# Conv-branch eviction and gate steps re-placed, final norm rearranged, in a one-core hybrid decoder layer

## Chip, core and metric

The program runs on one core of one Trainium2 chip. The metric is device time in microseconds (us) of one execution; lower is better. All 256 tokens (plus 16 learned meta tokens, 272 rows) go through one layer of width 2048 in one launch.

## What is computed

Cut to what matters here, the reference is:

```python
s = concat([meta, x])                                   # 272 x 2048
s = s + 0.5 * swiglu_ffn(rms_norm(s, g1), w_gu, w_down)
h = rms_norm(s, g_mix)
q, k, v, b_gate, c_gate, u = split(h @ w_in)
y_att  = diff_attention(q, k, v, ...)
y_conv = b_gate * short_conv(c_gate * u, conv_w)        # 3 taps along the tokens
z = [y_att @ w_branch[0], y_conv @ w_branch[1]]
s = s + (sum(sigmoid(h @ w_gate) * z)) @ w_out
s = s + 0.5 * swiglu_ffn(rms_norm(s, g2), w_gu, w_down)
out = rms_norm(s, norm_final)[16:]                      # 256 x 2048, fp32
```

## The kernel before, in words

Every large product is done in three fp32r products on TensorE (PE): each weight block is loaded by a DMA (`st`), cast to a high part `wh` on ScalarE (ACT, line 275 or 378), and the rest `wl = st - wh` is formed on VectorE (DVE, line 276 or 379). PE multiplies `wh` with the activation's high and low part and `wl` with its high part. `wh` and `wl` have three buffers each, `st` five. One block is two chunks of 128 rows in `linear` (line 248) and one chunk in `linear_tok` (line 314).

`linear` and `linear_tok` run a list of chunks. What else has to be done is put between the chunks by lists: `pending` holds the eviction of the product before and is emptied after chunk `EVICT_AT = 1` (`flush`); `side` holds small steps, one of which is taken at each chunk of `side_at`; `after` is called after each chunk. The order in which the text calls these is not yet the order on an engine: the framework schedules the instructions, and each engine then runs its own queue strictly in the order of the built program.

The part around the change:

- Lines 842 to 873, the conv branch in two groups `g` of 512 columns. For each group three `linear` calls run: `c`, `u`, `b`, eight blocks each, with `side_at=(3, 6, 9, 12)`. `c` and `u` have 258 token columns and three products per weight tile (lines 287 to 289); `b` has 256 and two (line 285 with 512 columns for both activation parts, line 289 with 256).
- `u_evict` (line 851) multiplies `u` into `cg` and forms the three taps into `yv`: per column tile `j` one multiplication (853), one scaling (855), two multiply-adds (857), four tiles in all, 16 DVE instructions. It runs at the flush in `b`.
- `side` holds the attention at that time: 18 steps of units (`scores`, `turn`, `values`), the norm and eight `att_out` steps (lines 800 to 813: two transposes on PE, line 808, a scaling on DVE, line 809; after every fourth tile a `split` of `yf` into `ya`, lines 173 and 174).
- `hg.renorm` (line 435) makes the activation of the gate from the residual `s`: two DVE instructions (440), then `pair`: an ACT copy (450), a DVE subtraction (451), and for pairs of kind `S` four DVE sums (455 to 458), an ACT copy (460) and a DVE subtraction (461). In group 1 it is called in `u` and `b` after chunks 3, 7, 11 and 15.
- Lines 927 to 992, the final norm. `down` (975) runs for each token half `i` and column quarter (`u`, `q`): add to `sT` (978), square with a sum into `fss` (982, ACT), multiply by the gain (983). In the last `linear_tok` (`hold = 3`) the products of half 1 come last. After the fourth quarter of a half, `finish(i)` (930) sums the four squares (933), scales (935), forms the inverse root by `rsqrt` (lines 222 to 230, the root on ACT) and scales the two column halves, one on ACT (941) and one on DVE (943), each followed by a store of 128 x 1024 issued by SyncE (SP, 944).

Of the kernel before, what the change touches and what calls it, by code (L numbers as in the profile page):

```python
# [22 lines left out]
GC = 4  # L23
GW = GC * P
W2 = D // 2
NH = 8
HD = 64
EPS = 1e-6
# [17 lines left out]
def decoder_layer(ctx: ExitStack, tc: tile.TileContext, t, out):  # L46
    nc = tc.nc

    const = ctx.enter_context(tc.tile_pool(name="const", bufs=1))
# [8 lines left out]
    def wide(shape, name):  # L58
        return tmp.tile(shape, F32, tag="wide", bufs=4, name=name)
# [31 lines left out]
    G_MIX, G_FFN2, G_CONV, G_SUB = 0, DC, 2 * DC, NV - 1  # L91

    def load_gain(g0, src):
# [5 lines left out]
        out=vrows[G_CONV:G_SUB, :], in_=t["conv_w"][0].rearrange("k (c p) -> (k c) p", p=P)  # L99
# [3 lines left out]
    for i, n in enumerate(("lambda_q1", "lambda_k1", "lambda_q2", "lambda_k2")):  # L103
# [7 lines left out]
        out=mask[:, T - P :],  # L111
        in_=mask[:, T - P :],
# [13 lines left out]
    def col(i):  # L126
        return vec[:, i : i + 1]
# [94 lines left out]
    def rsqrt(out_, ms, shape, name):  # L222

        a = tmp.tile([P, T], F32, tag="rsa", bufs=1, name="rsa" + name)[:, : shape[1]]
        nc.scalar.activation(a, ms, AF.Sqrt)
        nc.vector.reciprocal(out_, a)
        nc.vector.tensor_mul(a, out_, out_)
        nc.vector.tensor_mul(a, a, ms)
        nc.vector.tensor_scalar(a, a, -0.5, 1.5, op0=ALU.mult, op1=ALU.add)
        nc.vector.tensor_mul(out_, out_, a)  # L230
# [4 lines left out]
    side = []  # L235
# [174 lines left out]
    def gated_plain(norm, m, gi):  # L410


        def f(acc):
            mt = wide([P, 2, GW], "mt")
            for i in range(2):
                r = norm.rtok[:, i : i + 1]
                silu = tmp.tile([P, GW], F32, tag="sc", name="silu")
                nc.scalar.activation(silu, acc[i][0], AF.Silu, scale=r)
                nc.vector.scalar_tensor_tensor(
                    out=mt[:, i, :], in0=acc[i][1], scalar=r, in1=silu, op0=ALU.mult, op1=ALU.mult  # L420
                )
            for k in range(2):
                later.append(lambda k=k: back(m, 2 * gi + k, mt, k))

        return f
# [413 lines left out]
    nu = T - n0  # L839
    yc = Act("yc", NH, SEQ)  # L840
    hg = Mixed(norm2, G_MIX)
    for g in range(2):
        cg = wide([P, GC, T], "cg")
        yv = apool.tile([P, GC, SEQ], F32, tag="act", name=f"yv{g}")

        def c_evict(ps, cg=cg):
            for j in range(GC):
                nc.vector.tensor_mul(cg[:, j, :nu], ps[j][:, :nu], norm2.rstd[:, n0:])
                nc.vector.tensor_mul(cg[:, j, :nu], cg[:, j, :nu], norm2.rstd[:, n0:])

        def u_evict(ps, cg=cg, yv=yv, g=g):
            for j in range(GC):
                nc.vector.tensor_mul(cg[:, j, :nu], ps[j][:, :nu], cg[:, j, :nu])
                taps = [col(G_CONV + k * NH + g * GC + j) for k in range(3)]
                nc.vector.tensor_scalar_mul(yv[:, j, :], cg[:, j, 0:SEQ], taps[0])
                for k in (1, 2):
                    nc.vector.scalar_tensor_tensor(
                        out=yv[:, j, :], in0=cg[:, j, k : k + SEQ], scalar=taps[k], in1=yv[:, j, :],
                        op0=ALU.mult, op1=ALU.add,
                    )  # L860

        def b_evict(ps, yv=yv, g=g):
            for j in range(GC):
                nc.vector.tensor_mul(yv[:, j, :], yv[:, j, :], norm2.rstd[:, NMETA:])
                nc.vector.tensor_mul(yv[:, j, :], total(ps[j], SEQ), yv[:, j, :])
            split(yc, g, yv)

        kw = dict(side_at=(3, 6, 9, 12))
        linear(h2, allk, w_in, 0, 4 * W2 + g * GW, n0, T, "c", c_evict, **kw)
        for i, (m0, t0, nm, evict) in enumerate(((5 * W2, n0, "u", u_evict), (3 * W2, NMETA, "b", b_evict))):  # L870
            if g == 1:
                kw["after"] = lambda k, i=i: hg.renorm(4 * i + k // 4) if k % 4 == 3 else None
            linear(h2, allk, w_in, 0, m0 + g * GW, t0, T, nm, evict, **kw)
    while side:
        side.pop(0)()
# [26 lines left out]
    sT = [[apool.tile([P, W2], F32, tag="act", name=f"sT{i}{q}") for q in range(2)] for i in range(2)]  # L902
# [27 lines left out]
    def finish(i):  # L930

        ssq = const.tile([P, 1], F32, name=f"fssq{i}")
        nc.vector.tensor_reduce(out=ssq, in_=fss[:, i, :], axis=AX.X, op=ALU.add)
        fms = const.tile([P, 1], F32, name=f"fms{i}")
        nc.vector.tensor_scalar(fms, ssq, 1.0 / D, EPS, op0=ALU.mult, op1=ALU.add)
        fr = const.tile([P, 1], F32, name=f"fr{i}")
        rsqrt(fr, fms, [P, 1], f"f{i}")
        for q in range(2):
            y = sT[i][q]
            if q:  # L940
                nc.scalar.mul(y, y, fr)
            else:
                nc.vector.tensor_scalar_mul(y, y, fr)
            nc.sync.dma_start(out=out[i * P : (i + 1) * P, q * W2 : (q + 1) * W2], in_=y)

    w_gu, w_down = t["ffn2_w_gu"][0], t["ffn2_w_down"][0]
    hn = Mixed(norm3, G_FFN2)
# [8 lines left out]
    for half in thirds:  # L956
        m = Act("m", len(half) * GC, SEQ)
        for gi, g in enumerate(half):
            if g == 0:
                linear_tok(  # L960
                    [(h3, 0, w_gu, 0), (h3, 0, w_gu, F)], allk, 0, "pg", gated_plain(norm3, m, gi),
                    side_at=range(16), after=renorm_after,
                )
            else:
                gate_up_mix(hn, w_gu, g, m, gi)
        final = half is thirds[-1]
        if final:
            for q in range(2):
                nc.gpsimd.dma_start(
                    out=gfin[q],  # L970
                    in_=t["norm_final"][q * W2 : (q + 1) * W2].rearrange("(o d) -> o d", o=1).to_broadcast([P, W2]),
                )
        for u in range(2):

            def down(i, q, ps, u=u, final=final):
                fs = slice(q * GW, (q + 1) * GW)
                v = sT[i][u][:, fs]
                nc.vector.scalar_tensor_tensor(out=v, in0=ps, scalar=0.5, in1=v, op0=ALU.mult, op1=ALU.add)
                if final:
                    k = u * 2 + q  # L980
                    sq = wide([P, GW], "fsq")
                    nc.scalar.activation(sq, v, AF.Square, accum_out=fss[:, i, k : k + 1])
                    nc.vector.tensor_mul(v, v, gfin[u][:, fs])
                    if k == 3:
                        finish(i)

            hold = HOLD if final and u else 0
            linear_tok(
                [(m, 0, w_down, u * W2 + q * GW) for q in range(2)], list(range(len(half) * GC)), half[0] * GC, "pd",
                down if hold else lambda acc, down=down: [down(i, q, acc[i][q]) for q in range(2) for i in range(2)],  # L990
                hold=hold,
            )
# [26 lines left out]
```

## Time and profile before

| | |
|---|---|
| time, median of 3 runs | 2208.49 us (2207.37 to 2209.04) |
| the profiled execution's own time | 2207.09 us |
| its span, first to last instruction | 2205.3 us |
| PE busy | 2187.7 us (99%) |
| DVE busy | 1467.6 us (67%) |
| ACT busy | 1042.1 us (47%) |
| mean granted TensorE clock | 0.998 |

The profiled execution lies 1.8 us above its span; that part is outside the first and last instruction. A row of the timeline has start in us from the span's start, duration, engine, line, operation, output and inputs, a count where equal neighbours are merged, and in brackets how long the engine had been idle and what released it. "PEclk" is the TensorE clock that was granted, 1.00 being full. SPq is the queue in which SP issues DMAs.

### The profile page before, as it was taken

To read this page: it belongs to the slowest core of one execution; us is meant where nothing else is said; L and a number is where in the kernel's file an instruction comes from. 1 tells how busy PE (TensorE), PEld (TensorE's weight loads), DVE (VectorE), ACT (ScalarE), POOL (GpSimd) and SP (SyncE) were. 2 spreads that over 40 slices of the span, in tenths; PEclk is the share of its full clock that TensorE was granted. 3 is DMA by queue.
4 is the path that set the end of the run, shared out by engine and by line. 5 is a ranking of instruction groups with operands and counts; after the bars stand their busy time and mean duration, and the time that the engine had idled before them with its cause. 6 is when DMAs were issued, how large, how long until landed. Compare 5 with 4: busy or idle time off the path is not lost.

```text
span 2205.3 us, 33210 instructions
## 1 busy us (share of the span) xinstructions
PE 2187.7 (99%) x13534; PEld 1974.6 (90%) x13534; DVE 1467.6 (67%) x1903; ACT 1042.1 (47%) x1299; POOL 6.4 (0%) x17
## 2 busy tenths in 40 slices
PE   9999999999999999999999999999999999999997
PEld 8999999999999999898988888888888888888886
DVE  7555554445555565567787777678886688846985
ACT  6343433334333443444555555455554455534554
POOL 0000000000000000000000000000000000000000
PEclk9999999999999999999999999999999999999999
DMA  8555555555555555444535656554566455665562
GB/s 272 173 173 172 175 177 179 177 172 173 173 175 176 181 175 172 157 150 134 173 134 205 214 192 215 186 186 143 195 220 210 158 201 203 222 209 184 181 226 96
DMA packets 192105, 401.96 MB, mean 182 GB/s; under 512 B 8660, under 2 KB 8848, under 8 KB 191952
## 3 DMA queue, kind: packets, MB, share of 16 engines
q1 hardware_dynamic: 191232, 398.49, 53.3%
q8 instruction: 105, 1.72, 0.3%
q0 software_dynamic: 544, 1.21, 0.2%
q14 instruction: 48, 0.39, 0.0%
q10 hardware_dynamic: 176, 0.14, 0.0%
HBM read 397.71 MB, written 2.10 MB: 181 GB/s over the span
## 4 chain that ended last, share of the span: by engine, by line
PE 96%; DVE 1%; ACT 1%; DMA 1%; issue 0%; SPq 0%; DVEq 0%; ACTq 0%
PE pg L487 5%; PE pg L485 5%; PE pg L486 5%; PE pu L289 4%; PE pd L289 4%; PE pd L287 4%; PE pu L287 4%; PE pd L288 4%; PE pu L288 4%; PE pg L289 4%; PE pg L287 4%; PE pg L288 4%; PE pd L329 4%; PE pd L327 4%; PE pd L328 4%; PE o L285 3%
## 5 line engine op out<-in xcount | busy, mean ns | idle before, releaser
L276 DVE TENSOR_TENSOR wl<-st,wh 128x1024 fp32r<-128x1024 f32 x392 | 479.0, 1224 | 454.5 <-ACT wh L275 453.9
L275 ACT CAST wh<-st 128x1024 fp32r<-128x1024 f32 x392 | 411.2, 1050 | 607.3 <-PE pd L288 146.9
L378 ACT CAST wh<-st 128x1024 fp32r<-128x1024 f32 (+1 forms) x360 | 359.2, 1004 | 379.1 <-PE pd L328 128.7
L379 DVE TENSOR_TENSOR wl<-st,wh 128x1024 fp32r<-128x1024 f32 (+1 forms) x360 | 414.2, 1157 | 136.9 <-ACT wh L378 136.5
L287 PE MATMUL pg<-h,wh 128*128 128x272 f32 x704 | 202.9, 289 | 0.8 <-ACT wh L275 0.7
L287 PE MATMUL pu<-h,wh 128*128 128x272 f32 x704 | 203.1, 289 | 0.0
L289 PE MATMUL pd<-m,wl 128*128 128x272 f32 x704 | 203.0, 288 | 0.0
L289 PE MATMUL pu<-h,wl 128*128 128x272 f32 x704 | 203.0, 288 | 0.0
L287 PE MATMUL pd<-m,wh 128*128 128x272 f32 x704 | 202.9, 288 | 0.0
L288 PE MATMUL pu<-h,wh 128*128 128x272 f32 x704 | 202.4, 288 | 0.0
L288 PE MATMUL pd<-m,wh 128*128 128x272 f32 x704 | 202.4, 287 | 0.0
L288 PE MATMUL pg<-h,wh 128*128 128x272 f32 x704 | 201.7, 287 | 0.0
L289 PE MATMUL pg<-h,wl 128*128 128x272 f32 x704 | 200.6, 289 | 0.9 <-DVE wl L276 0.9
L485 PE MATMUL pg<-wh,hn 128*128 128x512 f32 x390 | 152.8, 392 | 0.0
L486 PE MATMUL pg<-wh,hn 128*128 128x512 f32 x390 | 151.9, 390 | 0.0
L487 PE MATMUL pg<-wl,hn 128*128 128x512 f32 x390 | 151.8, 392 | 0.0
L327 PE MATMUL pd<-wh,m 128*128 128x512 f32 x352 | 137.6, 391 | 0.0
L328 PE MATMUL pd<-wh,m 128*128 128x512 f32 x352 | 137.0, 389 | 0.0
L379 DVE TENSOR_TENSOR wl<-tt,wh 128x1024 fp32r<-128x1024 f32 x84 | 101.3, 1222 | 53.7 <-ACT wh L378 50.0
L329 PE MATMUL pd<-wl,m 128*128 128x512 f32 x352 | 136.9, 390 | 0.0
L287 PEld LDWEIGHTS pg<-h,wh 128*128 128x128 f32 x704 | 132.2, 188 | 1.4 <-ACT wh L275 1.4
L288 PEld LDWEIGHTS pg<-h,wh 128*128 128x128 f32 x704 | 132.8, 189 | 0.0
(299 smaller groups left out, 4729.3 us busy)
## 6 DMA issues: line engine op xcount, KB each, us to landing
st<-in_ffn_w_gu_dram SPq DMA_DIRECT2D x184, 512.0 KB, 4.3
st<-in_ffn_w_down_dram SPq DMA_DIRECT2D x88, 1024.0 KB, 5.1
st<-in_ffn_w_gu_dram SPq DMA_DIRECT2D x84, 1024.0 KB, 4.9
st<-in_w_in_dram SPq DMA_DIRECT2D x48, 1024.0 KB, 5.1
st<-in_w_gate_dram SPq DMA_DIRECT2D x64, 512.0 KB, 4.4
st<-in_w_branch_dram SPq DMA_DIRECT2D x32, 512.0 KB, 4.8
st<-in_w_out_dram SPq DMA_DIRECT2D x16, 1024.0 KB, 5.0
xin<-in_x_dram SPq DMA_DIRECT2D x8, 256.0 KB, 8.1
```

The lines of the kernel that those rows point to most:

```text
L275: nc.scalar.copy(out=wh[:, :m, :], in_=sw)
L276: nc.vector.tensor_sub(wl[:, :m, :], sw, wh[:, :m, :].bitcast(F32))
L287: nc.tensor.matmul(a, wh[:, i, f], act.part(c, 0, t0, t1), start=first, stop=False)
L288: nc.tensor.matmul(a, wh[:, i, f], act.part(c, 1, t0, t1), start=False, stop=False)
L289: nc.tensor.matmul(a, wl[:, i, f], act.part(c, 0, t0, t1), start=False, stop=last)
L327: nc.tensor.matmul(ps, hi, wh[:, q, :], start=first, stop=False)
L328: nc.tensor.matmul(ps, lo, wh[:, q, :], start=False, stop=False)
L378: nc.scalar.copy(out=wh, in_=src)
L379: nc.vector.tensor_sub(wl, src, wh.bitcast(F32))
L485: nc.tensor.matmul(ps[k], hi, wh, start=first, stop=False)
L486: nc.tensor.matmul(ps[k], lo, wh, start=False, stop=False)
L487: nc.tensor.matmul(ps[k], hi, wl, start=False, stop=left[k] == 0)
```

## The change

1. `u_evict` does column tiles 0 and 1 at the flush, and puts tiles 2 and 3 at the front of `side`, so that they are taken at chunk 3 of `b`, in the place of the attention step that stood there. All later steps of `side` move back by one slot in each group.
2. `hg.renorm` is called after chunks 4, 7, 10 and 13, for the same pairs in the same order.
3. Final norm: the sum of three of the four quarters and its scaling are done after the third quarter (`finish_part`); after the fourth, one instruction adds its part. A root of one column is taken early, in the eviction of the linear before (`k == 1`, half 1). The product of the last quarter with the gain goes to a new tile `fy`. The chain after the root has one instruction less in front of the scaling on DVE, which takes two scalars. Half 1 is scaled and stored in four pieces of 128 x 512 in place of two of 128 x 1024; those scaled on ACT are issued from ACT's queue.

```diff
         def u_evict(ps, cg=cg, yv=yv, g=g):
-            for j in range(GC):
-                nc.vector.tensor_mul(cg[:, j, :nu], ps[j][:, :nu], cg[:, j, :nu])
...
+            def taps(j0):
+                for j in (j0, j0 + 1):
+                    nc.vector.tensor_mul(cg[:, j, :nu], ps[j][:, :nu], cg[:, j, :nu])
...
+            taps(0)
+            side.insert(0, lambda: taps(2))
...
-                kw["after"] = lambda k, i=i: hg.renorm(4 * i + k // 4) if k % 4 == 3 else None
+                kw["after"] = lambda k, i=i: hg.renorm(4 * i + k // 3 - 1) if k in (4, 7, 10, 13) else None
...
+    fpart = const.tile([P, 2], F32, name="fpart")
+    fr = const.tile([P, 2, 4], F32, name="fr")
+
+    def finish_part(i):
+
+        nc.vector.tensor_reduce(out=fr[:, i, 3:4], in_=fss[:, i, 0:3], axis=AX.X, op=ALU.add)
+        nc.vector.tensor_scalar(fpart[:, i : i + 1], fr[:, i, 3:4], 1.0 / D, EPS, op0=ALU.mult, op1=ALU.add)
+
+    def finish(i, last):
+
+        ms, a, r, n = (fr[:, i, k : k + 1] for k in range(4))
+        nc.vector.tensor_scalar(ms, fss[:, i, 3:4], 1.0 / D, fpart[:, i : i + 1], op0=ALU.mult, op1=ALU.add)
+        nc.scalar.activation(a, ms, AF.Sqrt)
+        nc.vector.reciprocal(r, a)
+        nc.vector.scalar_tensor_tensor(out=n, in0=r, scalar=ms, in1=r, op0=ALU.mult, op1=ALU.mult)
+        nc.vector.tensor_scalar(n, n, -0.5, 1.5, op0=ALU.mult, op1=ALU.add)
+        nc.vector.tensor_mul(a, r, n)
+        rows = out[i * P : (i + 1) * P, :]
+        for u, q in ((0, 1), (0, 0), (1, 0), (1, 1)) if i else ((0, None), (1, None)):
+            cs = slice(0, W2) if q is None else slice(q * GW, (q + 1) * GW)
+            on_act = q == 0 or (q is None and u == 0)
+            y = last if u and q else sT[i][u][:, cs]
+            if on_act:
+                nc.scalar.mul(y, y, a)
             else:
-                nc.vector.tensor_scalar_mul(y, y, fr)
-            nc.sync.dma_start(out=out[i * P : (i + 1) * P, q * W2 : (q + 1) * W2], in_=y)
+                nc.vector.tensor_scalar(y, y, r, n, op0=ALU.mult, op1=ALU.mult)
+            eng = nc.scalar if on_act and i else nc.sync
+            eng.dma_start(out=rows[:, u * W2 + cs.start : u * W2 + cs.stop], in_=y)
...
-                    nc.vector.tensor_mul(v, v, gfin[u][:, fs])
+                    y = wide([P, GW], "fy") if k == 3 and i else v
+                    nc.vector.tensor_mul(y, v, gfin[u][:, fs])
+                    if k == 1 and i:
+
+                        nc.scalar.activation(fr[:, i, 3:4], fss[:, i, 1:2], AF.Sqrt)
+                    if k == 2:
+                        finish_part(i)
                     if k == 3:
-                        finish(i)
+                        finish(i, y)
```

More of the change, by code (lines that the diff above doesn't have):

```diff
@@ L851, in u_evict @@
         def u_evict(ps, cg=cg, yv=yv, g=g):
-            for j in range(GC):
[L853 to L860, printed above, removed]
+            def taps(j0):
+                for j in (j0, j0 + 1):
+                    nc.vector.tensor_mul(cg[:, j, :nu], ps[j][:, :nu], cg[:, j, :nu])
+                    w = [col(G_CONV + k * NH + g * GC + j) for k in range(3)]
+                    nc.vector.tensor_scalar_mul(yv[:, j, :], cg[:, j, 0:SEQ], w[0])
+                    for k in (1, 2):
+                        nc.vector.scalar_tensor_tensor(
+                            out=yv[:, j, :], in0=cg[:, j, k : k + SEQ], scalar=w[k], in1=yv[:, j, :],
+                            op0=ALU.mult, op1=ALU.add,
+                        )
+            taps(0)
+            side.insert(0, lambda: taps(2))
         def b_evict(ps, yv=yv, g=g):
```

11 lines of the change are left out of this document (removed).

## The prediction, made before the changed kernel was run

> **What bounds the kernel now.** I read the page's busy shares first, then PE's waits, then the timeline around the longest wait, then the end of the span.
>
> ```profile
> PE 2187.7 (99%) x13534; PEld 1974.6 (90%) x13534; DVE 1467.6 (67%) x1903; ACT 1042.1 (47%) x1299; POOL 6.4 (0%) x17
> ```
> ```profile
> PE b L289 <- DVE wl L276: 2.3, 1, 2.3
> PE pg L289 <- DVE wl L276: 0.9, 2, 0.6
> ```
> PE is busy all the time, so only PE's idle time, its clock and what lies behind its last product can be won or lost. One wait stands out: in `b` a product waits 2.3 us for a `wl`. No other wait behind the start is longer than 0.6 us. The timeline around it (PE, DVE and ACT rows):
>
> ```profile
> 1097.04 1.05 ACT L275 CAST wh<-st 128x1024 fp32r<-128x1024 f32 x1 [2.05 <-PE u L288]
> 1098.13 1.23 DVE L276 TENSOR_TENSOR wl<-st,wh 128x1024 fp32r<-128x1024 f32 x1 [1.88 <-ACT wh L275]
> 1101.04 0.69 DVE L451 TENSOR_TENSOR hn<-hnf,hn 128x512 fp32r<-128x512 f32 x1
> 1101.35 1.05 ACT L275 CAST wh<-st 128x1024 fp32r<-128x1024 f32 x1
> 1101.65 0.69 DVE L461 TENSOR_TENSOR sp<-sums,sp 128x512 fp32r<-128x512 f32 x1
> 1101.80 0.28 PE L287 MATMUL u<-h,wh 128*128 128x258 f32 x1
> 1102.25 0.76 DVE L853 TENSOR_TENSOR cg<-u,cg 128x258 f32<-128x258 f32 x2
> 1102.76 0.28 PE L289 MATMUL u<-h,wl 128*128 128x258 f32 x1
> 1102.89 0.39 PE L285 MATMUL b<-h,wh 128*128 128x512 f32 x1
> 1105.68 1.10 PE L285 MATMUL b<-h,wh 128*128 128x512 f32 x4
> 1107.80 1.22 DVE L276 TENSOR_TENSOR wl<-st,wh 128x1024 fp32r<-128x1024 f32 x1
> 1109.07 0.74 PE L289 MATMUL b<-h,wl 128*128 128x256 f32 x4 [2.29 <-DVE wl L276]
> ```
> ```profile
> 1106.78:1109.07 2.29, 0.00 (x1) 0.00 (x1) 2.29 (x5) 0.09 (x1) 0.00 (x0) 1.00 0.00 0
> 1110.14:1113.55 3.41, 3.41 (x13) 2.82 (x12) 3.41 (x6) 1.41 (x3) 0.00 (x0) 0.50 0.84 299
> 1113.55:1117.00 3.45, 3.45 (x21) 3.03 (x20) 2.67 (x6) 1.63 (x2) 0.00 (x0) 1.00 0.89 299
> ```
> The windows have length, then busy us of PE, PEld, DVE, ACT and POOL, then granted clock, DMA share and GB/s. DVE works without a pause from 1101.04: a renorm's rest, then the whole `u_evict` from 1102.25 to 1107.80 (5.55 us), and only then the `wl` of `b`'s second block. PE stands for 2.29 us, and shortly after runs 3.41 us at half the clock, which loses half of that, 1.71. Together **4.0 us**. The count of products agrees: eight pairs take 1105.68 - 1102.89 = 2.79 us, 0.349 each; the twelfth pair of `b`'s second and third block would start at 1105.68 + 11 x 0.349 = 1109.52 and starts at
>
> ```profile
> 1113.64 0.40 PE L285 MATMUL b<-h,wh 128*128 128x512 f32 x1
> ```
> that is 4.1 later. The end of the span:
>
> ```profile
> 2193.76 1.28 ACT L225 ACT_TABLE_LOAD   x1
> 2194.38 0.68 DVE L978 SCALAR_TENSOR_TENSOR sT<-pd,sT 128x512 f32<-128x512 f32 x1
> 2195.16 0.61 ACT L982 ACTIVATE fsq<-sT 128x512 f32<-128x512 f32 x1
> 2195.68 0.19 ACT L982 ACTIVATION_READ_ACCUMULATOR fsq<-sT 128x1 f32 x1
> 2196.61 0.15 DVE L933 TENSOR_REDUCE fssq<-fss 128x1 f32<-128x4 f32 x1
> 2196.73 0.75 DVE L943 TENSOR_SCALAR sT<-sT,fr 128x1024 f32<-128x1024 f32 x1
> 2197.51 3.08 SPq L944 DMA_DIRECT2D out_dram<-sT  x4
> 2198.97 1.15 ACT L941 ACTIVATE sT<-sT,fr 128x1024 f32<-128x1024 f32 x1 [1.00 <-DVE fr L230]
> 2199.75 0.84 SPq L944 DMA_DIRECT2D out_dram<-sT  x2
> ```
> ```profile
> 2198.37:2203.71 5.34, 0.00 (x0) 0.00 (x0) 1.23 (x4) 1.15 (x1) 0.00 (x0) 0.56 0.98 393
> ```
> From 2198.37 to 2203.71 the DMA engines are 98% busy: 2.10 MB go out in one unbroken stream of 5.34 us, although the last store is issued only near 2200.2. So the end is set by **when the first store starts** (2197.51, 0.86 before the stream) and by the stream's length, not by the chain of half 1.
>
> **The change part by part.**
>
> *u_evict in two parts, renorm moved.* No work goes; DVE's order changes. In the order of the changed program tiles 2 and 3 stand right behind tiles 0 and 1: the split leaves no gap in DVE's queue. What moves is the `wl` of `b`'s second block: renorm and `ya` no longer stand ahead of it, so it comes *before* `u_evict`, and the third block's `wl` comes behind. I lay this out from t, the start of `b`. A block of `u` has 24 products of 0.12 us (1101.80 to 1102.76 is eight of them), 2.88. The cast of `b`'s second block waits for a buffer that PE frees when the last block of `u` begins, at t - 2.80; cast 1.05, `wl` 1.23, so `u_evict` can start at t - 0.57. It takes 5.55, and the third `wl` runs from t + 4.98 to t + 6.20, seen by PE at t + 6.25. PE begins the third block at t + 5.58 and in the new order does its four wide products first (1105.68 to 1106.78 by their row, 0.91 until the next can start): t + 6.49. So 0.24 us are left: tight, but no stall. For the block behind, DVE has one L451 (0.69) and one `wl`: ready at t + 8.0, needed at t + 8.6. Gain: the 4.0 us, if no new stall replaces them.
>
> *Attention one slot later.* In group 0 the step that lay in `b` before the third block now comes within it. Rows of group 0:
>
> ```profile
> 1033.71 1.21 DVE L276 TENSOR_TENSOR wl<-st,wh 128x1024 fp32r<-128x1024 f32 x1
> 1034.05 0.48 PE L780 MATMUL po<-vA,aA 16*128 16x128 f32 x2
> 1034.46 0.71 PE L782 MATMUL po<-vN,aB 128*128 128x128 f32 x4
> 1035.98 0.50 PE L285 MATMUL b<-h,wh 128*128 128x512 f32 x1
> 1036.32 0.28 PE L289 MATMUL b<-h,wl 128*128 128x256 f32 x1
> ```
> The `wl` behind `u_evict` is there at 1034.92 and PE needs it at 1036.32: 1.4 of cover, because 1.93 us of attention (1034.05 to 1035.98) lie ahead. In the new order PE has four wide products (0.91) and one L780 (1034.05 to 1034.46, 0.41) ahead: 1035.37, cover 0.4. PE's queue holds all later products behind that one, and the evictions of `b` wait for them. The steps themselves cost PE the same; the last one falls into `b` of group 1, at 12 slots per group no step is left over. What the new neighbourhoods of transposes and `scores` cost is not in the trace: at least 0 (no work added), at most 0.6, the longest small wait above. I take **0.2**, since the covers I found are positive but small. Over both groups the bounds stay 0 and 0.6.
>
> *Early root.* One root and its table load move into the last `linear_tok`. ACT waits there 1.67 us before every cast:
>
> ```profile
> 2153.20 1.05 ACT L378 CAST wh<-st 128x1024 fp32r<-128x1024 f32 x1 [1.67 <-PE pd L328]
> ```
> 1.28 + 0.20 fits in that; without it PE would wait up to 1.5. At the old place the load was almost hidden as well: it ended at 2195.04, and the last square started at 2195.16, 0.10 behind its input (2194.38 + 0.68).
>
> *Partial sums and root.* PE's last product is where it was. DVE now has a reciprocal and a reduce of half 0 and 1 ahead of the last L978: 0.15 later. The square's sum is then ready at 2196.0. In the new order the scaling of half 1's sum, which waits for this, stands *ahead* of half 0's last multiplication on DVE: 2196.05, then 2196.2, then half 0's DVE scaling (0.75) from 2196.3 to 2197.05. First store at 2197.1 against 2197.51: **0.4 won**, in spite of that wait. If DVE with two scalars is as slow as L276 (1.22 for the same size), nothing is won; I take L943, the same operation with one scalar. Half 0's ACT piece (1.15) follows by 2197.55, and half 1's four pieces are issued between 2198.2 and 2199.9 while half 0's 2.67 us of stream run until about 2200.6, so the stream doesn't break.
>
> *Quarters from two queues.* Half 1's pieces have rows of 2 KB where 4 KB were. The page has, for mostly 2 KB packets,
>
> ```profile
> q1 hardware_dynamic: 191232, 398.49, 53.3%
> ```
> 53.3% of 16 x 2205.3 us over 191232 packets is 98 ns each; a 4 KB packet of the stores takes 16 x 0.98 x 4096 B / 393 GB/s = 163 ns. 512 packets of 98 ns on 16 engines are 3.1 us against 2.67: at most 0.5 lost, at least 0. I take **0.1**, near the lower end, since the 98 ns are a mean with packets that met others. The second queue wins nothing while the engines are full. The Trainium skill, page "DMA: Bandwidth & Descriptors", section "Rules for kernel authors", says that spreading DMAs over issuing engines doesn't help since all run on the same 16 engines. By that rule this part gives 0; with a bandwidth of its own for the second queue it would give the fourth rival's time.
>
> **The sum.** -4.0 + 0.2 - 0.4 + 0.1 = -4.1 us. On the profiled execution 2207.09 becomes 2203.0; on the median of the runs, 1.4 higher, 2208.49 becomes **2204.4** (-0.19%). A measurement of this kernel can tell about 0.2%, 4.4 us, from no change, so the forecast lies just inside that bound.
>
> **Rivals.**
>
> *The half clock stays.* Only the wait goes, and the 3.41 us at half clock belong to something else: -2.29 + 0.2 - 0.3 = -2.4, **2206.1**. For it: PE had run again for 1.07 us when the clock fell. Against: it is the only such window between the start and PE's end, and it follows the only long wait. The Trainium skill, page "TensorE: Matmul & The Clock Gate", section "Part 1: The HAM clock gate", has the clock halve after an idle window of about 3.4 us, free-running; 2.29 us of idle would be too short by that, which speaks for this rival, while the length of 3.41 us agrees. Chance 0.11.
>
> *The stall finds another place.* One block of the same group waits over 2 us and the clock falls again: only the tail's 0.3 is won, **2208.2**. Chance 0.06.
>
> *Slower: `u_evict`, still one run of 5.55 us, stalls PE in both groups.* The place is the third block of `b`. The covers are 0.24 and 0.4; if the `wl` behind it comes 2.3 us or more beyond the cover (two further DVE steps of the renorm or attention ahead of it), each group pays 4.0: 2208.49 + 4.0 - 0.3 = **2212.2**. It decides from about 2 us of idle, since the trace shows no half clock behind the 0.6 waits. Against it: the new order has nothing between. Chance 0.06.
>
> *The stores aren't bound by the engines.* Then the last issue counts: ACT's second store at about 2199.45 against 2200.18, and its half size (1.33 us of stream becomes 0.67): 1.4 won, -4.0 + 0.2 - 1.4 = -5.2, **2203.3**. Against it stands the 98%. Chance 0.10.
>
> **How the numbers follow.** The forecast has 0.67. Its own range is 2203.6 to 2205.4 (covers 0 to 0.6, tail from -0.4 to +0.5), and about two fifths of it lie below 2204.07, the bound of 0.2%. Faster: 0.27 + 0.10 = 0.37. Slower: the third rival, 0.06. The same: 0.57. The range of 8 in 10 goes from 2203.2 to 2206.5: it takes in the first and the fourth rival and leaves out the two with a stall.
>
> **What would show it.** No PE wait over 1 us for `wl` in `b`, and clock 1.00 in every window there (stall and clock); the third block's `wl` behind `u_evict` in both groups with PE waiting under 0.5 (covers); the table load in the last `linear_tok` with no PE wait behind it; the first store 0.4 earlier counted from PE's last product, DMA share again about 0.98 until the last landing, and a stream of 5.3 to 5.8 us. A clock of 0.50 anywhere between the start and PE's end makes the prediction wrong by 1.7 at least; a break in the store stream makes the tail's term wrong.

## The result, and the profile after

| | before | changed |
|---|---|---|
| time, median of 20 runs each | 2208.50 us (2206.74 to 2211.43) | 2204.57 us (2203.64 to 2207.28) |
| the profiled execution's own time | 2207.09 us | 2203.69 us |
| its span | 2205.3 us | 2201.9 us |
| TensorE's (PE's) last end to the last landing | 9.87 us | 9.65 us |

The ratio is 0.9983, with a 95% interval from 0.9977 to 0.9989: 3.9 us faster, between 2.4 and 5.1. The forecast was 2204.4.

The first part of the page after, busy us of each engine: the work is the same but for one VectorE (DVE) and two ScalarE (ACT) instructions.

```profile
PE 2186.8 (99%) x13534; PEld 1973.6 (90%) x13534; DVE 1467.6 (67%) x1904; ACT 1041.3 (47%) x1301; POOL 6.4 (0%) x17
```

PE's longest wait behind the start, after (us in total, times, longest). The 2.3 us in `b` are gone, and no wait of `b` has taken their place:

```profile
PE pg L289 <- DVE wl L276: 0.9, 2, 0.6
```

The window after, over the part of group 1 where the stall was (length; busy PE, PEld, DVE, ACT, POOL; granted clock, DMA share, GB/s): PE busy throughout, clock 1.00.

```profile
1106.00:1109.50 3.50, 3.50 (x22) 3.04 (x21) 3.50 (x7) 1.36 (x2) 0.00 (x0) 1.00 0.09 33
```

DVE's timeline after, group 1. The `wl` of `b`'s second block (1100.72) now stands ahead of `u_evict`, the third block's behind it (1107.40):

```profile
1100.72 1.23 DVE L276 TENSOR_TENSOR wl<-st,wh 128x1024 fp32r<-128x1024 f32 x1 [0.36 <-ACT wh L275]
1101.86 0.76 DVE L854 TENSOR_TENSOR cg<-u,cg 128x258 f32<-128x258 f32 x2
...
1107.40 1.23 DVE L276 TENSOR_TENSOR wl<-st,wh 128x1024 fp32r<-128x1024 f32 x1
```

ACT's queue has moved as well. Before, the cast of this block started at 1101.35, behind the casts L173, L450 and L460, 1.54 us ahead of `b`'s first product (1102.89); it ended at 1102.40, so with this order on ACT the `wl` couldn't have started ahead of `u_evict` (1102.25). After, it starts 2.74 us ahead of that product (1102.37):

```profile
1099.63 1.05 ACT L275 CAST wh<-st 128x1024 fp32r<-128x1024 f32 x1 [1.63 <-PE u L288]
```

Where did the 3.4 us between the two profiled executions come from? I cut PE's time at products that both have: the first of `pu` near the start, the last of `u` in group 1, the first of the gate's `g`, the last of the kernel. PE's timeline of the kernel before (its row of `u` at 1102.76 stands in the prediction), and then after:

```profile
39.15 0.49 PE L287 MATMUL pu<-h,wh 128*128 128x272 f32 x1
1129.42 0.40 PE L485 MATMUL g<-wh,hn 128*128 128x512 f32 x1
2193.80 0.39 PE L329 MATMUL pd<-wl,m 128*128 128x512 f32 x1
```
```profile
38.86 0.49 PE L287 MATMUL pu<-h,wh 128*128 128x272 f32 x1
1102.25 0.28 PE L289 MATMUL u<-h,wl 128*128 128x258 f32 x1
1125.03 0.40 PE L485 MATMUL g<-wh,hn 128*128 128x512 f32 x1
2190.53 0.39 PE L329 MATMUL pd<-wl,m 128*128 128x512 f32 x1
```

| stretch | before | after | difference |
|---|---|---|---|
| start to `pu` | 39.15 | 38.86 | -0.29 |
| `pu` to the last `u` | 1063.61 | 1063.39 | -0.22 |
| last `u` to the gate | 26.66 | 22.78 | **-3.88** |
| gate to PE's last product | 1064.38 | 1065.50 | +1.12 |
| that product's start to the span's end | 11.5 | 11.4 | -0.1 |

The stall's stretch gave 3.9 us; 1.1 seem to be given back behind it. Experiment 3 takes them up.

The tail after, DVE, ACT and the queues that issue stores (SPq, ACTq):

```profile
2190.38 0.19 ACT L946 ACTIVATE fr<-fr 128x1 f32<-128x1 f32 x1
2190.51 0.69 DVE L1001 TENSOR_TENSOR sT<-sT,gfin 128x512 f32<-128x512 f32 x1 [0.67 <-ACT fsq L999]
...
2192.71 0.21 DVE L945 TENSOR_SCALAR fr<-fss,fpart 128x1 f32<-128x1 f32 x1
2192.91 0.81 DVE L959 TENSOR_SCALAR sT<-sT,fr 128x1024 f32<-128x1024 f32 x1
2193.74 1.66 SPq L961 DMA_DIRECT2D out_dram<-sT  x3
2195.21 1.49 ACTq L961 DMA_DIRECT2D out_dram<-sT  x2
2195.50 1.14 SPq L961 DMA_DIRECT2D out_dram<-fy  x1
```
```profile
2194.60:2200.13 5.53, 0.00 (x0) 0.00 (x0) 0.74 (x2) 1.19 (x2) 0.00 (x0) 0.60 1.00 379
```

Half 0's root (2190.38) comes without a table load. The first store is issued 2193.74 - 2190.92 = 2.82 us behind PE's last end (3.32 before), and from 2194.60 the engines are full (1.00) for 5.53 us, again to the end.

### The profile page after: what moved, and what is told of

It is laid out like the page before. It is cut to its first block, busy times and chain, and to the rows that moved or that the text cites. A ratio compares the mean times of both kernels' runs of the same rounds, so it can differ in the third digit from the quotient of the medians.

```text
span 2201.9 us, 33218 instructions
## 1 busy us (share of the span) xinstructions
PE 2186.8 (99%) x13534; PEld 1973.6 (90%) x13534; DVE 1467.6 (67%) x1904; ACT 1041.3 (47%) x1301; POOL 6.4 (0%) x17
## 4 chain that ended last, share of the span: by engine, by line
PE 97%; DVE 1%; ACT 1%; DMA 0%; issue 0%; SPq 0%; DVEq 0%; ACTq 0%
PE pg L487 5%; PE pg L485 5%; PE pg L486 5%; PE pu L289 4%; PE pd L289 4%; PE pd L287 4%; PE pu L287 4%; PE pu L288 4%; PE pd L288 4%; PE pg L289 4%; PE pg L287 4%; PE pg L288 4%; PE pd L329 4%; PE pd L327 4%; PE pd L328 4%; PE o L285 3%
```

## The experiments

Three things were to be told apart: which of the edits moves the `wl`, what the stall costs and why the clock falls, and what sets the end of the tail. Single executions differ by 2 us for reasons outside the change (experiment 3), and the interval of a ratio reaches 1.3 to 2 us to each side, so the verdicts rest on stretches of the traces. In the runs beside these kernels the kernel before had medians from 2207.71 to 2208.62 us.

### 1. Which edit moves the `wl`

**The later slot alone** (the kernel before, with an empty step at the front of `side`; `u_evict` whole):

```diff
+            side.insert(0, lambda: None)
```

> The kernel before, with u_evict whole as it was, renorm where it was and the old final norm; the one edit is an empty step at the front of the side list at each u_evict, so that attention stands one slot later. In the built order the `wl` of b's second block (group 1) then comes ahead of u_evict. Theory (order): what removes the stall is that the `wl` passes u_evict, and the later attention step does that; so the 2.29 us wait goes, one L451 (0.69) is left behind u_evict ahead of the next `wl`, so PE waits about 0.4 there; no half clock; 3.4 to 4.0 us faster than before. Rival (parts): the evicting in two parts is what matters; then the wait of 2.3 and the half clock stay and the time is that of before. Rival (renorm): the later renorm matters; the same, time of before.

**The two parts alone:**

```diff
-            for j in range(GC):
...
+            taps(0)
+            side.insert(0, lambda: taps(2))
```

> The kernel before with u_evict in two parts alone; renorm and final norm as before. In the built order both parts stand behind each other on DVE. Theory (order): the same as with the empty step, a wait of about 0.4, clock 1.00, 3.4 to 4.0 us faster than before. Rival (parts): about 4 us faster while the empty step alone gives nothing. Rival (renorm): no faster than before.

**The renorm's places alone:**

```diff
-                kw["after"] = lambda k, i=i: hg.renorm(4 * i + k // 4) if k % 4 == 3 else None
+                kw["after"] = lambda k, i=i: hg.renorm(4 * i + k // 3 - 1) if k in (4, 7, 10, 13) else None
```

> The kernel before with the renorm steps after chunks 4, 7, 10, 13 alone. In the built order the L451 and L461 of the fourth pair and a `ya` still stand between the `wl` of b's first block and u_evict, and the second block's `wl` behind it. Theory (order): the 2.3 us wait stays, with a stretch of half clock behind it; the time of before within 0.7 us. Rival (renorm): the wait goes, about 4 us faster. Rival (half clock from elsewhere): a wait of 2.3 without a stretch of half clock, or the stretch at another place.

**The final norm alone** (the third part of the change on the kernel before):

```diff
-    def finish(i):
...
+    def finish_part(i):
...
+    def finish(i, last):
...
```

> The kernel before with the new final norm alone. Theory (the stores' stream is set by its first store and the DMA engines): stall and half clock as before; from PE's last product to the end of the span 0.1 to 0.4 us less than the 11.13 of before; the time 0.1 to 0.4 us less, which a timing cannot tell from none. Rival (the stores aren't bound by the engines): 1.4 us less behind PE's last product.

| | median, us | ratio to before | PE's wait in `b` | last `u` to the gate |
|---|---|---|---|---|
| later slot alone | 2205.26 | 0.9986 [0.9978, 0.9995] | none | 23.02 |
| two parts alone | 2205.04 | 0.9986 [0.9977, 0.9995] | none | 23.0 |
| renorm alone | 2209.69 | 1.0006 [0.9997, 1.0014] | 2.3 | 26.7 |
| final norm alone | 2206.80 | 0.9996 [0.9988, 1.0005] | 2.3 | 26.7 |
| the whole change | 2204.57 | 0.9983 [0.9977, 0.9989] | none | 22.78 |

DVE's timeline with the later slot alone:

```profile
1103.25 1.23 DVE L276 TENSOR_TENSOR wl<-st,wh 128x1024 fp32r<-128x1024 f32 x1 [0.36 <-ACT wh L275]
1104.39 0.75 DVE L853 TENSOR_TENSOR cg<-u,cg 128x258 f32<-128x258 f32 x2
...
1109.95 0.68 DVE L451 TENSOR_TENSOR hn<-hnf,hn 128x512 fp32r<-128x512 f32 x1
1110.55 2.35 DVE L276 TENSOR_TENSOR wl<-st,wh 128x1024 fp32r<-128x1024 f32 x2
```

and with the renorm alone:

```profile
1100.56 0.69 DVE L174 TENSOR_TENSOR ya<-yf,ya 128x512 fp32r<-128x512 f32 x1 [0.69 <-ACT ya L173]
...
1102.37 0.75 DVE L853 TENSOR_TENSOR cg<-u,cg 128x258 f32<-128x258 f32 x2
...
1107.92 2.35 DVE L276 TENSOR_TENSOR wl<-st,wh 128x1024 fp32r<-128x1024 f32 x2
```

An *empty* step does nearly all of it: `u_evict` still runs in one piece of 5.6 us, and the `wl` comes ahead of it. The split of `u_evict` is not what wins, except that it fills the slot. With the renorm moved alone, the `wl` stays behind. What the slot moves is an attention step with its `split`, and L174 with its ACT cast (L173) no longer stands ahead at that place; that this `split` and not the slot's other work decides it is read from the order only, it wasn't tried by itself. ACT's queue fits: with the slot alone the second block's cast (1102.17) no longer stands behind L173 and L450, with the renorm alone (1101.47) it still does. Expected with the slot alone was a wait of about 0.4 at the third block; the list of waits has none, and the stretch is 0.24 longer. By the medians it is 3.36 us faster, the two parts 3.58, where 3.4 to 4.0 were expected. The renorm's move does take the L451 (1109.95) out from between `u_evict` and the third block's `wl`; beside the slot that is 23.02 - 22.78 = 0.24 us. Alone it changes nothing that could be told (its interval holds 1, and its stretch is before's). The final norm alone shortens the tail from 9.87 to 9.63 us, too little for its interval.

### 2. What a wait at that place costs

**More work ahead of the third block's `wl`** (the changed kernel; in group 1 the taps of tiles 2 and 3 are formed twice, with the same values):

```diff
+            def rest():
+                taps(2)
+                if g == 1:
+                    for j in (2, 3,):
...
-            side.insert(0, lambda: taps(2))
+            side.insert(0, rest)
```

> The changed kernel, with the taps of the third and fourth tile of conv group 1 worked out once more behind the later part (about 2.1 us more of DVE work ahead of the third block's wl; the same values again). In the changed kernel this wl is 0.23 us early, so TensorE should wait 1.8 to 1.9 us at that block in either theory. What the wait costs: (A) the clock follows any wait as long as about 2 us: a stretch of 3.41 us at 0.50 behind it, 3.6 us in all. (B) the clock is set in stretches of 3.41 us on a fixed grid, and halves for the next stretch where TensorE stood for more than some 1.5 us of one of them (idle 1.39 and 1.41 us of a stretch were not followed by 0.50, 1.75 us at the start of the kernel with the shifted slot alone was): then a wait of 1.85 us halves the clock only if it falls nearly whole into one stretch, and the trace shows by the grid whether it does; cut by a boundary into pieces under 1.4 us it costs 1.85 us alone. Time 2206.4 (B, cut) to 2208.2 (A).

Time 2205.29 us in one run, under the 2206.4 to 2208.2 that were expected; its stretch behind the gate was a quick one (1064.45 us, see experiment 3). PE's timeline at the wait and two windows of this kernel:

```profile
1109.58 0.38 PE L808 MATMUL yt<-ident,oN 128*128 128x128 f32 x2
1111.46 0.74 PE L289 MATMUL b<-h,wl 128*128 128x256 f32 x4 [1.50 <-DVE wl L276]
```
```profile
1107.60:1111.02 3.42, 2.37 (x14) 1.76 (x12) 3.42 (x9) 1.05 (x1) 0.00 (x0) 1.00 0.00 0
1111.02:1114.43 3.41, 2.97 (x18) 2.67 (x19) 3.41 (x7) 0.92 (x1) 0.00 (x0) 1.00 0.08 10
```

PE waits 1.50 us, not 1.85, since two transposes (0.38) that stood elsewhere now come ahead of the product; and the clock stays at 1.00. From the last `u` to the gate it takes 24.55 us, 1.77 more than the changed kernel. So the cover of the third block is as thin as the prediction had it: 2.1 us of added DVE work cost 1.8. A wait of this length costs about itself. Theory B holds here, but a wait of 1.5 us is too far from 2.3 for this run alone to refute A.

### 3. The kernel before, once more

> The kernel before once more, for what changes from run to run. The wait of 2.3 us at the second block of b must be there again. If the clock halves for a stretch of a fixed grid of 3.41 us behind one in which TensorE stood for over half of it, the 0.50 stretch follows unless a boundary of the grid cuts the wait into pieces of under some 1.5 us (about 1 case in 3); if any such wait halves the clock, it follows at once. Drift: from the wait to TensorE's last end the kernel before takes within 0.5 us of the first profile's if that part is the same from run to run, and the 1.1 us that the changed kernel gave back between 1130 and 2033 us is then its own; a difference of 1 us between two runs of this one kernel says that it is noise.

Time 2211.47 us in one run. Its windows at the stall and behind it, and its PE rows:

```profile
1107.96:1111.37 3.41, 1.11 (x6) 0.58 (x5) 3.41 (x8) 1.05 (x1) 0.00 (x0) 1.00 0.00 0
1111.37:1114.79 3.42, 3.42 (x13) 3.04 (x14) 3.42 (x6) 0.62 (x2) 0.00 (x0) 0.50 0.71 219
```
```profile
41.30 0.49 PE L287 MATMUL pu<-h,wh 128*128 128x272 f32 x1
1104.92 0.28 PE L289 MATMUL u<-h,wl 128*128 128x258 f32 x1
1131.59 0.40 PE L485 MATMUL g<-wh,hn 128*128 128x512 f32 x1
2198.03 0.39 PE L329 MATMUL pd<-wl,m 128*128 128x512 f32 x1
```

The stretch from `u` to the gate takes 26.67 us (26.66 in the first profile), the one before it 1063.62 (1063.61): both repeat within 0.01 us. The other two don't: `pu` starts 2.15 us later, and from the gate to the last product it takes 1066.44 us against 1064.38. One and the same kernel differs by 2.1 us behind the gate, and the changed kernel's 1065.50 lies between. Over all traces this stretch takes 1064.38 to 1066.54 us in the four without the later slot and 1064.45 to 1066.01 in the ten with it. So **nothing shows that the change gave 1.1 us back**: the first profile of before was quick in a stretch that varies. Why it varies stays open.

### 4. What sets the end

All that follows are variants of the changed kernel. A table first; times are counted from PE's last end, landings are those of the DMA records.

| kernel | first store issued | half 1's last store issued | stream | last landing |
|---|---|---|---|---|
| before | 3.32 | 6.00 | 5.34 | 9.87 |
| changed | 2.82 | 4.90 | 5.53 | 9.65 |
| without the early root | 3.20 | 5.08 | 5.54 | 10.09 |
| half 0's multiplication first | 1.74 | 5.50 | 5.73 | 8.91 |
| half 1 in two halves | 2.28 | 5.03 | 5.36 | 8.84 |
| both of these | 1.73 | 5.49 | 5.88 | 8.82 |
| half 0's chain first | 0.44 | 5.54 | 7.22 | 8.87 |
| the same, half 1's eviction next | 0.44 | 4.92 | 6.61 | **8.25** |

This measure repeats: the four other traces with the old final norm (before again, later slot, two parts, renorm) give 9.87 to 9.89, the two others with the new one (final norm alone, more work) 9.63 and 9.69.

**Without the early root:**

```diff
-                    if k == 1 and i:
...
-                        nc.scalar.activation(fr[:, i, 3:4], fss[:, i, 1:2], AF.Sqrt)
```

> The changed kernel without its early root, so that the table for the root is loaded in the tail, ahead of half 0's root. If the load is hidden (the prediction's step): half 0's multiplication on DVE starts about where it does now, 2.0 us after TensorE's last end, first store within 0.2 us of 2.8 us after it, last landing 9.6 us after it. Rival: the load stands between square and root on ACT, half 0's root is 1.3 us later, and with it first store and last landing 0.7 to 1.3 us later.

ACT and DVE in its tail:

```profile
2191.22 1.28 ACT L946 ACT_TABLE_LOAD   x1
2192.52 0.20 ACT L946 ACTIVATE fr<-fr 128x1 f32<-128x1 f32 x1
2194.02 0.81 DVE L959 TENSOR_SCALAR sT<-sT,fr 128x1024 f32<-128x1024 f32 x1
```

The load is partly hidden: half 0's multiplication starts 2.36 us behind PE's last end in place of 1.99, and the last landing is 0.44 later. The root itself comes 1.40 us later (0.86 behind PE's last end in place of 0.54 ahead of it), but DVE's queue would have kept the multiplication back for most of that anyway.

**Half 0's multiplication first** (order on DVE: half 1's last two products with the gain behind it):

```diff
-                nc.vector.tensor_scalar(y, y, r, n, op0=ALU.mult, op1=ALU.mult)
+                scaled.append(nc.vector.tensor_scalar(y, y, r, n, op0=ALU.mult, op1=ALU.mult).ins)
...
-                    nc.vector.tensor_mul(y, v, gfin[u][:, fs])
+                    with ExitStack() as order:
+                        if k >= 2 and i:
+                            order.enter_context(tc.issue_after(scaled[0]))
+                        nc.vector.tensor_mul(y, v, gfin[u][:, fs])
```

> The changed kernel, with the last two products with the gain of half 1 put behind the multiplication of half 0 by its root on DVE. In the changed kernel this multiplication starts at 2192.91 us, behind one product (0.68) and the small steps of half 1's root. Theory (the stream of the output's packets sets the end, and it starts with half 0's first store): multiplication from about 2192.05, first store about 0.85 us earlier against TensorE's last end, stream unbroken (half 1's quarters are ready about 2195.0 to 2195.7, before the 2.7 us of half 0's packets are through), so from TensorE's last end to the last landing 8.8 us in place of 9.65. Rival (half 1's chain sets the end): its product is 0.7 us later, the stream has a gap of that size before the quarters, and 9.65 us stay.

**Half 1 in two halves**, from SyncE's queue alone. Both quarters of its second column half go to one new tile, so the product of the third quarter is no longer written in place:

```diff
+                    if k == 2 and i:
+                        fy2.append(wide([P, 2, GW], "fy"))
+                    y = fy2[0][:, q, :] if u and i else v
...
+            elif (u, q) in ((0, 0), (1, 1)):
+                y = fy2[0].rearrange("p q f -> p (q f)") if u else sT[1][0]
+                nc.sync.dma_start(out=rows[:, u * W2 : (u + 1) * W2], in_=y)
```

> The changed kernel, with half 1 stored as two halves of 128x1024 from SP alone (4 KB rows) in place of four quarters of 2 KB rows from two queues. Theory (the engines are full, and a 2 KB packet of 88 ns costs more per byte than a 4 KB packet of 166 ns): the stream takes 5.35 us in place of 5.53, from TensorE's last end to the last landing 0.1 to 0.2 us less. Rival (two queues feed the engines better, or the quarters are ready sooner): a gap in the stream before half 1's first packet, stream 5.6 us or more.

**Both of these:**

> The two edits before this one together: half 0's multiplication ahead of half 1's last products, and half 1 in two halves from SP. If the stream sets the end: first store 0.85 us earlier, stream 5.35 us, from TensorE's last end to the last landing 8.65 us in place of 9.65, time about 1.0 us under the changed kernel's (2203.5), 0.9977 to 0.9979 of the kernel before. If half 1's chain sets it, now that its halves must be whole before they are stored: a gap of 0.3 to 0.7 us in the stream, and little or nothing of that.

The streams of the three, in this order:

```profile
2195.82:2201.56 5.74, 0.00 (x0) 0.00 (x0) 2.06 (x8) 1.54 (x3) 0.00 (x0) 0.62 0.96 365
```
```profile
2193.97:2199.34 5.37, 0.00 (x0) 0.00 (x0) 1.35 (x5) 1.33 (x2) 0.00 (x0) 0.50 0.99 391
```
```profile
2193.73:2199.62 5.89, 0.00 (x0) 0.00 (x0) 2.06 (x8) 1.73 (x5) 0.00 (x0) 0.67 0.90 356
```

Half 0's multiplication first gave 0.74 us in place of 0.85, and the stream has its first idle time (0.96). Two halves gave 0.81 where 0.1 to 0.2 were expected: the stream shrank as expected (5.36), but the first store also came 0.54 earlier. The cause stands in DVE's and ACT's rows of this kernel, beside those of the changed kernel above:

```profile
2189.68 0.63 ACT L1003 ACTIVATE fsq<-sT 128x512 f32<-128x512 f32 x1 [1.42 <-DVE sT L999]
2189.68 0.69 DVE L1007 TENSOR_TENSOR fy<-sT,gfin 128x512 f32<-128x512 f32 x1
2192.29 0.81 DVE L960 TENSOR_SCALAR sT<-sT,fr 128x1024 f32<-128x1024 f32 x1
```

In the changed kernel the third quarter's product (2190.51) overwrites what the square reads, so DVE stands 0.67 us until the square is done, and half 0's root chain stands behind it. Written to another tile, the product starts beside the square. With half 0's multiplication first, where this product stands elsewhere, DVE is idle for the same 0.67 us, until the sum that the next step needs is there; so the new tile fills the wait with work. Tile and halves weren't tried apart: that the earlier first store comes from the tile is read from these rows. Both edits together win nothing over the two halves alone: the first store is 0.55 earlier still, but half 1's stores are 0.47 later, and the stream has a gap (0.90). The bound has moved from the stream to half 1's chain. Its median of 2203.30 us (ratio 0.9981 [0.9972, 0.9990]) lies 4.4 us under before's.

**Half 0's chain first** (two halves kept; the sum, root and reciprocal of half 0 ahead of half 1's evictions and products on DVE, its root ahead of half 1's squares on ACT):

```diff
+                with behind(dve[1] if late else None):
+                    nc.vector.scalar_tensor_tensor(out=v, in0=ps, scalar=0.5, in1=v, op0=ALU.mult, op1=ALU.add)
...
+                    with behind(act[0] if late else None):
+                        nc.scalar.activation(sq, v, AF.Square, accum_out=fss[:, i, k : k + 1])
...
+                    with behind(dve[2] if late else dve[0] if k == 3 else None):
+                        nc.vector.tensor_mul(y, v, gfin[u][:, fs])
```

> The version with half 1 in two halves, and half 0's chain (sum, root, reciprocal, refinement, multiplication) put ahead of half 1's evictions and products on DVE, and its root ahead of half 1's squares on ACT. Half 0's last squares end 2.6 us before TensorE's last end in the changed kernel, but its root's chain stands on DVE behind an eviction and two products of 0.69 us. If queue order on DVE is what holds the first store: first store near TensorE's last end (0.5 us before to 0.5 us after it, in place of 2.8 us after), half 0's packets through 3.5 us after it, and then half 1's chain sets the end: first packet of half 1 about 4.6 to 5.2 us after TensorE's last end, 2.7 us of packets, last landing 7.6 to 8.2 us after it, in place of 9.65 in the changed kernel and 8.8 with the halves alone; time 1.4 to 2.0 us under the changed kernel's (about 2202.8). Rival: the root's chain has a latency of its own (each small step waits for the one before, and the eviction of half 1 falls among them), half 0's first store not before 1.5 us after TensorE's last end, last landing 8.5 us or more.

The first store came 2.38 us earlier than in the changed kernel, within what was expected, but the end came no earlier than with the two halves alone: 8.87 against 8.84, where 7.6 to 8.2 were expected. The miss is half 1's chain. Its last eviction stood behind half 0's multiplication and its own third product, a product of 0.68 us that nobody waited for:

```profile
2191.97 0.81 DVE L964 TENSOR_SCALAR sT<-sT,fr 128x1024 f32<-128x1024 f32 x1
2192.76 0.68 DVE L1023 TENSOR_TENSOR fy<-sT,gfin 128x512 f32<-128x512 f32 x1
2193.42 0.68 DVE L1010 SCALAR_TENSOR_TENSOR sT<-pd,sT 128x512 f32<-128x512 f32 x1
```

Median 2203.49 us, ratio 0.9981 [0.9972, 0.9990].

**The same, with half 1's last eviction directly behind half 0's multiplication:**

```diff
-                with behind(dve[1] if late else None):
+                with behind(dve[2] if late and k == 3 else dve[1] if late else None):
...
+                    if late and k == 2:
+                        held.append((y, v, fs))
```

> The version before this one (half 0's chain first) with half 1's last eviction put directly behind half 0's multiplication on DVE, and its two products with the gain behind that eviction. If half 1's chain sets the end there, as its gap in the stream says: half 1's square and sum 0.5 to 0.6 us earlier, its two stores too, last landing 8.3 us after TensorE's last end in place of 8.87; the packets of half 0 (2.7 us, from about 1.3 us after TensorE's last end) are through before half 1's first, so that nothing is given back. If the stream or something else sets it: 8.8 us stay. Time by the median: about 0.5 us under the 2203.3 and 2203.5 of the two versions before, which the intervals of the times alone can't tell.

Its streams, half 0's, the gap, and half 1's:

```profile
2192.90:2195.58 2.68, 0.00 (x0) 0.00 (x0) 2.31 (x9) 1.15 (x4) 0.00 (x0) 1.00 0.99 390
2195.58:2196.78 1.20, 0.00 (x0) 0.00 (x0) 0.47 (x2) 0.92 (x2) 0.00 (x0) 0.96 0.06 24
2196.78:2199.51 2.73, 0.00 (x0) 0.00 (x0) 0.00 (x0) 0.00 (x0) 0.00 (x0) 0.50 0.95 374
```

8.25 us, as expected (8.3). With 1.2 us of empty engines between the halves, the end now hangs on half 1's chain alone. The median is 2203.07 us, ratio 0.9978 [0.9969, 0.9987]: the lowest of all, faster than both kernels by the traces (1.4 us of tail less than the changed one); the interval of the times alone overlaps with the changed kernel's.

## Why the prediction was right, step by step

**The stall and its clock, -4.0.** Right, and nearly the whole result: 3.88 us in that stretch. The clock is 1.00 from 7.80 us to behind PE's end, which refutes the first rival: the half clock belonged to the wait. No wait of `b` is left, so the second falls too.

**"The split leaves no gap ...; what moves is the `wl`".** Right. But its reason, "renorm and `ya` no longer stand ahead of it", is half wrong: moving the renorm does nothing for it (26.7 us stay), and the slot alone does it. The renorm's own share is 0.24 us, further back.

**The covers.** 0.24 us in group 1 were worked out; the rows give 0.23: PE's product that needs the third `wl` starts at 1108.91, and the `wl` ends at 1107.40 + 1.23 = 1108.63, with 0.05 to be seen. In group 0, 0.4 were worked out; there the `wl` runs from 1033.37 to 1034.59 and its product starts at 1035.06, 0.42 with the same 0.05. The experiment with added work shows that there is nothing else behind it: the third rival's mechanism exists, it was only 2 us of DVE work away.

**Attention one slot later, +0.2.** Wrong in sign, and small: from `pu` to the last `u`, PE takes 1063.39 to 1063.41 us in all traces with the later slot and 1063.58 to 1063.62 in the four without it. 0.2 us are won, where I took a price of 0.2 with a lower bound of 0. The bound was too strict: a step that moves can also leave a worse place.

**Early root.** Its cover in the last `linear_tok` held (no PE wait there). That the load was "almost hidden" at its old place was taken over into the new order, where it isn't: without the early root the tail is 0.44 longer. The new order of the tail is worth its 0.22 only together with the early root.

**First store, -0.4.** 3.32 to 2.82: 0.50. The chain is as worked out: half 1's sum stands ahead of half 0's multiplication (2192.71, 2192.91), which takes 0.81 with two scalars, where 0.75 were taken from the one-scalar row.

**Quarters from two queues, +0.1.** The stream is 0.19 longer. A 2 KB packet takes 87 to 88 ns, not the 98 of the estimate, and a 4 KB one 166 where it was 162: 512 packets of 88 ns and 256 of 166 over 16 engines are 2.82 + 2.66 = 5.48. The second queue shortens nothing: the engines are full (1.00) and the stream is no shorter, so the fourth rival falls. The Trainium skill, page "DMA: Bandwidth & Descriptors", section "Rules for kernel authors", says that spreading DMAs over issuing engines doesn't help, which agrees. Going back to two halves gives the 0.17 back.

**The sum.** -0.22 - 3.88 - 0.22 in the tail = -4.3 by the stretches that repeat, -4.1 predicted, -3.9 by the medians. That the total came within 0.2 is in part luck: the attention term is off by 0.42, the others by 0.1 each, and the interval of the measured time goes from 2.4 to 5.1. What didn't hold beyond this kernel: that the stream alone sets the end. It did here; but with half 1 in two halves, half 1's chain had only some 0.5 us to spare. There half 0's packets (2.67 us, from 3.13 behind PE's last end) are through at 5.80, and half 1's first store, issued at 4.41, brings its first packets at about 5.26, by the 0.85 that half 0's took (2.28 to 3.13). And DVE's wait for the square that it overwrites, 0.54 us of the first store by the rows of experiment 4, stood in the rows of before as well:

```profile
2193.78 0.69 DVE L983 TENSOR_TENSOR sT<-sT,gfin 128x512 f32<-128x512 f32 x1 [0.73 <-ACT fsq L982]
```


## What to carry to other kernels

When an engine with 67% load stalls the bound engine, look at the *order* of its queue at that place: an empty step in a list of work did as much as splitting the long piece. An operation that overwrites what another engine still reads is a wait in the middle of a strict queue; a new tile for its output cost no time here and let everything behind it go 0.5 us earlier. In a tail of two chains, each speed-up moves the bound to the other: read after each edit whether the stream is unbroken (then shorten it or start it earlier) or has a gap (then the later chain is the bound).

## What the runs showed of the hardware

**The clock is granted in stretches of 3.41 us on a grid, and about half of a stretch decides.** Changes of the clock lie whole multiples of 3.4133 us apart in each trace (7.63 and 1110.14 us before: 323 of them; 7.80 and 2195.74 after: 641), and the grid's place differs from one execution to the next. Windows laid on that grid, each with the clock that followed:

| execution | PE busy in the stretch, us of 3.41 | clock of the next |
|---|---|---|
| the four with the wait of 2.3 us, at that wait | 1.11 to 1.20 | 0.50 |
| before again, start | 1.30 | 0.50 |
| before again, at PE's end | 1.60 | **1.00** |
| later slot alone, start | 1.67 | 0.50 |
| half 0's multiplication first, start | 1.69 | 0.50 |
| half 1's eviction next, at PE's end | 1.75 | 1.00 |
| half 1's eviction next, start | 1.93 | 1.00 |
| changed, at PE's end | 2.01 | 1.00 |
| two parts alone, start, two stretches | 2.63 and 2.31 | 1.00 |
| more work, at the wait | 2.37 | 1.00 |

Half 0's multiplication first at its start, and the kernel before once more at PE's end:

```profile
12.62:16.03 3.41, 1.69 (x11) 1.47 (x12) 2.32 (x6) 2.23 (x5) 0.00 (x0) 1.00 1.05 393
16.03:19.44 3.41, 3.41 (x17) 3.41 (x16) 2.52 (x5) 1.99 (x4) 0.00 (x0) 0.50 1.05 387
```
```profile
2196.82:2200.23 3.41, 1.60 (x8) 0.98 (x6) 2.35 (x9) 2.82 (x6) 0.00 (x0) 1.00 0.00 0
2200.23:2203.64 3.41, 0.00 (x0) 0.00 (x0) 2.78 (x12) 1.68 (x3) 0.00 (x0) 1.00 0.31 126
```

Up to 1.30 us busy, 0.50 followed; from 1.75 on, 1.00. Between them the order isn't clean (1.60 kept the clock, 1.67 and 1.69 lost it), so the limit is near half a stretch, and busy time as the profile counts it is not exactly what decides. The grid explains why PE had run for 1.07 us when the clock fell: the stretch with the wait had first to end. The Trainium skill, page "TensorE: Matmul & The Clock Gate", section "Part 1: The HAM clock gate", gives the stretch as 3413 ns and free-running, which agrees; that it takes an idle window to lose the clock doesn't, since PE had worked up to half of one. A wait of 2.3 us should by this escape the half clock when a boundary of the grid cuts it well; in the four traces that have it, it lay nearly whole in one stretch each time, so this stays untested. The grid also accounts for part of what varies between executions: in the loads at the start (12 to 15 us) PE waits 0.7 to 2.3 us in all, and three of the 14 traces have one half-clock stretch there, which costs half of 3.41, 1.7 us. In these three `pu` starts at 41.24 to 41.38 us, in the others at 38.86 to 39.86.

**Issuing a store took longer with more stores in flight.** The last two issues of the changed kernel took 1.14 us (SPq) and 0.88 (ACTq), where its first four took 0.35 to 0.49; with half 0's multiplication first, where the same pieces are issued further into the stream, these two took 0.35 each. A queue without room would do this; no run shows its filling directly.
